# Moving layernorm and merge additions from GpSimd to VectorE, with another order in the third merge

## The chip, the cores and the metric

The kernel runs on one core of a Trainium2 chip. The metric is the device time of one execution in microseconds (us). A core has a matrix engine (TensorE, PE in the profile, with its weight loads as PEld), VectorE (DVE), ScalarE (ACT), GpSimd (POOL) and SyncE (SP), which here only issues transfers. Each engine works through its own queue in order and waits at semaphores for the others. All values are float32. The matrix products use a float32 form that rounds its operands, so the kernel splits each operand into a high and a low part and adds three products (high·high, low·high, high·low).

## The reference

One layer of a recurrent decoder with 512 prompt rows and 32 sample rows, which the kernel treats as 544 columns of one problem. What matters here, with the branches' own recurrences left out:

```
gates  = sigmoid(x @ w_in[gates] + b)                      # 3 branches x 1024
merged = gates[0]*(h_gla @ w_up_gla) + gates[1]*(h_ml @ w_up_ml) + gates[2]*(h_hg @ w_up_hg)
x = LN(2**0.25 * x + merged @ w_out;  ln1)
hid = square(relu(x @ w_ff_up))
x = LN(2**0.25 * x + hid @ w_ff_down; ln2)
LN(x) = (x - mean(x)) * rsqrt(mean((x - mean(x))**2) + 1e-5) * g + b     # over the 1024 channels
```

## The kernel before, in words

Everything is held transposed: channels lie on the 128 partitions, the 544 rows along them. A vector of 1024 channels is thus eight tiles of 128x544 (`KD = 8`), called column tiles below, and a product is computed one output tile at a time: `gemm` (line 160 on) loads the weight tile of 128x1024 by a transfer on SP's queue into `raw` (three buffers), ScalarE copies it to `wh` (line 141), VectorE subtracts to get `wl` (line 142; two buffers each of `wh` and `wl`), and PE runs 8 x 3 x 2 matmuls of 272 columns into one of two PSUM buffers (line 158). So one output tile of a product with 1024 channels is 48 matmuls, one of the third merge (256 channels) is 12, and one of the second feed-forward product (2 x 1024 channels per block) is 96. The `wh` of a product can be written only when the product two before it has stopped reading that buffer.

The inputs of the products are `xh`, `xl` (the layer's input, split), `mh`, `ml` (the merged branches), `x1h`, `x1l` (after the first layernorm) and the tiles `hid*`, `hd*` (the hidden layer). `xh`, `xl`, `x1h` and `x1l` are tiles [128, 8, TX] with TX = 546, so that two extra columns behind the 544 can carry the layernorm's gain and bias through the first feed-forward product; a row of one column tile has 2184 bytes. `mh` and `ml` have rows of 544 values, 2176 bytes.

The order of the instructions is set by a scheduler which simulates the program as it is written and gives some instructions (those under `high_priority`) precedence; each engine then keeps that order.

**Merges** (class `Merge`, lines 840 to 874). For each of eight tiles, `gates` computes a sigmoid gate: product (48 matmuls), bias on VectorE (line 215), three activations on ScalarE (lines 206 to 208). `products` computes the branch's projection; VectorE multiplies it with the gate (line 868) and GpSimd adds it to `merged` (line 872). The first merge writes instead of adding. The third one (line 935 on) computes all eight gates first, then all eight products, and splits each finished tile of `merged` into `mh` (ScalarE) and `ml` (VectorE, line 180), which the output projection reads next.

**Layernorm** (`ln_tile`, line 953). After each tile of the output projection VectorE adds the residual (line 1019 in the first layernorm; 1060 in the second, after the last feed-forward product). The sums over channels run over tiles: `a1` gathers x and `a2` its squares, and a matmul with a constant matrix then sums over the partitions (lines 985 and 992). To keep the numbers small, x is first centred on `cm`. Before the change `cm` is the mean over the first four tiles: GpSimd adds three of them (line 961), VectorE the fourth, a matmul (line 967) takes the mean; only then are the four tiles centred in one go (line 972, VectorE), squared (ScalarE, line 974) and added to `a1` and `a2` on GpSimd (lines 978 and 979). In the first layernorm each centred tile is also written as `x1h` (ScalarE, 1012) and `x1l` (VectorE, 1013) for the feed-forward product. In the second, the last two tiles are handled apart (lines 1063 to 1094) with the columns in two halves: their weights are split beforehand into `lh` and `ll` (line 180), the two tiles are centred before their product is added (line 1075).

**End** (lines 1097 to 1109). For each half of the columns the eight tiles get `ne` added (the negative mean), are multiplied by `rstd`, and get gain and bias. Tuples at the top give some of this to GpSimd (`ADDP`, `MULP`) and VectorE (`AFFD`), the rest to VectorE and ScalarE. Transfers of two tiles each go out on SP's queue. Between the two layernorms, during the first feed-forward product, GpSimd also applies the first layernorm to the residual (lines 1049 and 1050, sixteen additions and multiplications of 128x544).

Of the kernel before, what the change touches and what calls it, by code (L numbers as in the profile page):

```python
# [14 lines left out]
T = 544  # L15
# [4 lines left out]
TX = T + 2  # L20
# [9 lines left out]
ADDP, MULP, AFFD = (5, 6, 7), (7,), (2, 5)  # L30
# [12 lines left out]
def build(tc, I, O):  # L43
    nc = tc.nc
    with ExitStack() as ctx:
# [78 lines left out]
        ones5 = const.tile([128, 128], F32R, name="ones5")  # L124
        nc.gpsimd.memset(ones5.bitcast(F32), 1.0 / 512.0)
# [713 lines left out]
        class Merge:  # L839
# [7 lines left out]
            def gates(self, m0, pl):  # L847
                for m in range(m0, m0 + 4):
# [14 lines left out]
            def products(self, m0):  # L863
                for m in range(m0, m0 + 4):
# [6 lines left out]
                    eng = nc.gpsimd  # L871
                    eng.tensor_tensor(out=merged[:, m, :], in0=merged[:, m, :], in1=g, op=ALU.add)  # L872
# [58 lines left out]
        gb2s, gb2p = pool("gb2", 4)  # L931
# [4 lines left out]
        mr_.gates(0, gbp)  # L936
        mr_.gates(4, gb2p)
        mr_.split()
        mr_.products(0)
        mr_.products(4)  # L940
        gb2s.close()
# [11 lines left out]
        def ln_tile(x, m, sl, last, after):  # L953

            if m == 0:
                return
            if m < 4:
                eng = nc.vector if m == 3 else nc.gpsimd

                to = a1 if m < 3 else ftile("a1r").bitcast(F32R)  # L960
                eng.tensor_tensor(out=to[:, sl], in0=(x[:, 0, sl] if m == 1 else a1[:, sl]), in1=x[:, m, sl], op=ALU.add)  # L961
                if m < 3:
                    return
                for hf in range(2):
                    ps = psr.tile([128, 512], F32, tag="r", name="mu")
                    s = slice(hf * HT, (hf + 1) * HT)
                    nc.tensor.matmul(ps[:, 0:HT], ones5, to[:, s], start=True, stop=True)
                    nc.scalar.activation(out=cm[:, s], in_=ps[:, 0:HT], func=AF.Copy)
                nc.gpsimd.memset(a1, 0.0)
                nc.gpsimd.memset(a2, 0.0)  # L970
            for i in range(0 if m == 3 else m, m + 1):
                nc.vector.tensor_tensor(out=x[:, i, sl], in0=x[:, i, sl], in1=cm[:, sl], op=ALU.subtract)  # L972
                sq = ftile("sq")
                nc.scalar.activation(out=sq[:, sl], in_=x[:, i, sl], func=AF.Square)
                if after:
                    after(i, sl)
                eng = nc.vector if last else nc.gpsimd
                eng.tensor_tensor(out=a1[:, sl], in0=a1[:, sl], in1=x[:, i, sl], op=ALU.add)
                eng.tensor_tensor(out=a2[:, sl], in0=a2[:, sl], in1=sq[:, sl], op=ALU.add)
# [252 lines left out]
```

## Time and profile before

| | us |
|---|---|
| median of 3 runs (lowest, highest) | 968.91 (965.64, 971.26) |
| the profiled execution's own time | 968.76 |
| its span, from the first to the last instruction | 966.9 |
| PE busy | 926.0 (96%) |
| DVE busy | 569.1 (59%) |
| ACT busy | 404.5 (42%) |
| POOL busy | 232.9 (24%) |

The profile counts a matmul as busy from its start to its modelled end, and matmuls overlap: a 272-column matmul is given some 288 ns, but a new one starts about every 125 ns. A stretch in which PE is busy all the time can therefore still differ in how many matmuls it holds, and the useful figure is matmuls per stretch. Time is counted from the first instruction. The third merge's products lie at 472 to 489 us, the output projection and first layernorm at 489 to 549, the feed-forward products at 549 to 955, with the second layernorm from 870 on.

### The profile page before, as it was taken

The page shows a single profiled execution, that of the slowest core. Times are in us where ns is not written, and L with a number is a line of the kernel's source. Part 1 is how long each engine was busy: PE and PEld are TensorE (multiplying, and loading weights), DVE is VectorE, ACT ScalarE, POOL GpSimd, SP SyncE. Part 2 cuts the span into 40 slices and gives each one's busy share as a digit, 9 for nine tenths or more (in the row PEclk, how much of TensorE's full clock was granted, in tenths as well). Part 3 has the DMA queues.
Part 4 walks back from the last instruction along what each step waited for, and adds up shares of the span by engine and source line. Part 5 has one row for each costly group of instructions (what it writes and reads, how often), then busy time and mean ns, then how long its engine had stood idle before and what let it go on. Part 6 is the DMA issues. An engine that isn't in the chain of part 4 may idle for free.

```text
span 966.9 us, 17405 instructions
## 1 busy us (share of the span) xinstructions
PE 926.0 (96%) x7279; PEld 910.7 (94%) x7279; DVE 569.1 (59%) x877; ACT 404.5 (42%) x688; POOL 232.9 (24%) x210
## 2 busy tenths in 40 slices
PE   8999999799999999999989798999999999999795
PEld 7998999799999999999989798999999999999794
DVE  4895467866775676773565855553222455532836
ACT  4386223643555443545523356542111344521414
POOL 0311232643102435120235692000000000001722
PEclk9999999899999999999999899999999999999898
DMA  7321241022132112041144222222222222222202
GB/s 258 118 86 44 84 129 57 16 87 88 60 96 90 49 47 97 25 158 55 33 154 121 79 67 87 88 88 88 87 88 87 88 87 88 88 87 88 85 3 93
DMA packets 37598, 82.73 MB, mean 86 GB/s; under 512 B 12709, under 2 KB 18341, under 8 KB 37521
## 3 DMA queue, kind: packets, MB, share of 16 engines
q1 hardware_dynamic: 25072, 73.28, 23.3%
q10 hardware_dynamic: 12384, 8.33, 3.0%
q8 instruction: 57, 0.93, 0.4%
q14 instruction: 21, 0.16, 0.1%
q0 software_dynamic: 64, 0.02, 0.0%
HBM read 76.51 MB, written 5.09 MB: 84 GB/s over the span
## 4 chain that ended last, share of the span: by engine, by line
PE 86%; DVE 6%; POOL 3%; issue 2%; ACT 1%; DMA 1%; ACTq 0%; DVEq 0%
PE g L158 74%; PE g L83 3%; PE lv L401 2%; POOL merged L1050 2%; POOL merged L1049 1%; DVE wl L142 1%; DVE qe L393 1%; DVE merged L972 1%; PE o L458 1%; DVE x1l L1013 1%; PE oTm L760 1%; PE qkp L673 0%; PE oT L282 0%; DVE ml L180 0%; DMA fw<-in_wfirst 0%
## 5 line engine op out<-in xcount | busy, mean ns | idle before, releaser
L142 DVE TENSOR_TENSOR wl<-raw,wh 128x1024 fp32r<-128x1024 f32 (+2 forms) x139 | 168.4, 1212 | 152.4 <-ACT wh L141 149.6
L141 ACT ACTIVATE wh<-raw 128x1024 fp32r<-128x1024 f32 (+2 forms) x139 | 133.3, 959 | 277.0 <-PE g L158 258.8
L158 PE MATMUL g<-xh,wh 128*128 128x272 f32 x752 | 162.1, 295 | 0.0
L158 PE MATMUL g<-xh,wl 128*128 128x272 f32 x752 | 161.2, 293 | 0.0
L158 PE MATMUL g<-xl,wh 128*128 128x272 f32 x752 | 161.1, 294 | 0.0
L158 PEld LDWEIGHTS g<-xl,wh 128*128 128x128 f32 x752 | 120.8, 191 | 0.9 <-issue 0.5
L158 PEld LDWEIGHTS g<-xh,wh 128*128 128x128 f32 x752 | 121.0, 192 | 0.7 <-issue 0.2
L158 PEld LDWEIGHTS g<-xh,wl 128*128 128x128 f32 x752 | 121.1, 192 | 0.3
L158 PE MATMUL g<-x1h,wh 128*128 128x272 f32 (+1 forms) x512 | 107.1, 290 | 2.9 <-DVE relu L1036 2.9
L158 PE MATMUL g<-x1l,wh 128*128 128x272 f32 (+1 forms) x512 | 106.9, 290 | 0.0
L158 PE MATMUL g<-x1h,wl 128*128 128x272 f32 (+1 forms) x512 | 106.9, 290 | 0.0
L158 PEld LDWEIGHTS g<-x1h,wh 128*128 128x128 f32 x512 | 81.2, 189 | 3.3 <-DVE relu L1036 3.3
L158 PEld LDWEIGHTS g<-x1l,wh 128*128 128x128 f32 x512 | 81.5, 190 | 0.1
L158 PEld LDWEIGHTS g<-x1h,wl 128*128 128x128 f32 x512 | 80.8, 188 | 0.0
L961 POOL TENSOR_TENSOR a<-merged 128x544 f32<-128x544 f32 x2 | 4.8, 2421 | 295.6 <-ACT wh L141 284.3
L158 PE MATMUL g<-hidl,wh 128*128 128x272 f32 x280 | 58.1, 289 | 0.0
L158 PE MATMUL g<-hidh,wh 128*128 128x272 f32 x280 | 57.9, 288 | 0.0
L158 PE MATMUL g<-hidh,wl 128*128 128x272 f32 x280 | 57.8, 288 | 0.0
L1038 ACT ACTIVATE relu<-relu,gw 128x544 f32<-128x544 f32 x32 | 24.0, 750 | 77.2 <-DVE relu L1037 77.2
L872 POOL TENSOR_TENSOR merged<-merged,gb 128x544 f32<-128x544 f32 x16 | 26.8, 1678 | 86.8 <-ACT gb L207 47.8
L215 DVE TENSOR_SCALAR gb<-g,vec 128x544 f32<-128x544 f32 x24 | 18.8, 782 | 45.2 <-PE g L158 45.1
L158 PEld LDWEIGHTS g<-hidl,wh 128*128 128x128 f32 x280 | 44.0, 188 | 0.0
(405 smaller groups left out, 1863.3 us busy)
## 6 DMA issues: line engine op xcount, KB each, us to landing
raw<-in_wff SPq DMA_DIRECT2D x64, 512.0 KB, 3.6
raw<-in_win SPq DMA_DIRECT2D x47, 512.0 KB, 3.2
xr<-in_xT SPq DMA_DIRECT2D x16, 272.0 KB, 3.2
raw<-in_wout SPq DMA_DIRECT2D x8, 512.0 KB, 4.0
out_yT<-merged SPq DMA_DIRECT2D x8, 272.0 KB, 2.4
fw<-in_wfirst ACTq DMA_DIRECT2D x8, 256.0 KB, 5.4
raw<-in_wup_ml SPq DMA_DIRECT2D x8, 192.0 KB, 2.3
raw<-in_wup_gla SPq DMA_DIRECT2D x8, 192.0 KB, 2.4
```

The costliest lines, as they stand in the source:

```text
L83: nc.tensor.matmul(first_ps[i][hf], w[:, i * 128:(i + 1) * 128], a[:, k, hf * HT:(hf + 1) * HT], start=(k == 0 and n == 0), stop=(k == KD ...
L141: nc.scalar.activation(out=h[:, 0:n], in_=raw[:, 0:n], func=AF.Copy)
L142: nc.vector.tensor_tensor(out=l[:, 0:n], in0=raw[:, 0:n], in1=h[:, 0:n].bitcast(F32), op=ALU.subtract)
L158: nc.tensor.matmul(ps[:, hf, 0:w_], w, a(k)[:, hf * HT:hf * HT + w_], start=(k == 0 and s == 0), stop=(k == nk - 1 and s == 2))
L215: nc.vector.tensor_scalar(out, ps, vcol(col), XMIN, ALU.add, ALU.max)
L393: nc.vector.tensor_tensor(out=Q[s, :, p, 0:L // 2].rearrange("p a (n m) -> p a n m", m=m), in0=blk(qv)[s, :, :, m:2 * m], in1=Ev[s, :, :, ...
L401: nc.tensor.matmul(lv[0:R, o:o + 2 * H].rearrange("p (a b) -> p a b", a=2), Kv[:, p, c * R:(c + 1) * R], Q[:, p, :, c * H:(c + 1) * H], st ...
L458: nc.tensor.matmul(o[:, h * dv:(h + 1) * dv], at[:, c * 4 + h, :], vtok[:, cc, h * dv:(h + 1) * dv], start=(h == 0), stop=(cc == 0 and h = ...
L760: nc.tensor.matmul(oT[0:97, h * 32 + 4 * n:h * 32 + 4 * n + 4], Cs[:, n, :], qF[h][:, 4 * n:4 * n + 4], start=False, stop=(h == 3 and n == 7))
L872: eng.tensor_tensor(out=merged[:, m, :], in0=merged[:, m, :], in1=g, op=ALU.add)
L1038: nc.scalar.activation(out=r_, in_=r_, func=AF.Relu, bias=gw[:, 1:2])
L1050: nc.gpsimd.tensor_tensor(out=y, in0=y, in1=rstd, op=ALU.mult)
```

## The change

- Rows: TX goes from 546 to 548, so a row of `xh`, `xl`, `x1h`, `x1l` has 2192 bytes in place of 2184.
- Merges: the addition to `merged` is done by VectorE in place of GpSimd. The third merge computes the gate of tile m+1, then the product of tile m, and so on, in place of eight gates and then eight products. A pool of four more gate buffers goes.
- Layernorms: `cm` is the mean of the first tile alone (ScalarE copies it, a matmul with 1/128 takes the mean). Every tile is centred as soon as it is there. The additions to `a1` and `a2` are done by VectorE; the first tile starts the sums without an addition, so two memsets of GpSimd go.
- End: all additions and multiplications by VectorE, all gains and biases by ScalarE.

```
-TX = T + 2
+TX = T + 4
...
-ADDP, MULP, AFFD = (5, 6, 7), (7,), (2, 5)
+ADDP, MULP, AFFD = (), (), ()
...
-        nc.gpsimd.memset(ones5.bitcast(F32), 1.0 / 512.0)
+        nc.gpsimd.memset(ones7.bitcast(F32), 1.0 / 128.0)
...
-                    eng = nc.gpsimd
-                    eng.tensor_tensor(out=merged[:, m, :], in0=merged[:, m, :], in1=g, op=ALU.add)
+                    nc.vector.tensor_tensor(out=merged[:, m, :], in0=merged[:, m, :], in1=g, op=ALU.add)
...
-        mr_.gates(0, gbp)
-        mr_.gates(4, gb2p)
+        mr_.gates(0, gbp, 1)
         mr_.split()
-        mr_.products(0)
-        mr_.products(4)
-        gb2s.close()
+        for m in range(KD):
+            if m + 1 < KD:
+                mr_.gates(m + 1, gbp, 1)
+            mr_.products(m, 1)
...
-        def ln_tile(x, m, sl, last, after):
+        def ln_tile(x, m, sl, after):

             if m == 0:
-                return
-            if m < 4:
-                eng = nc.vector if m == 3 else nc.gpsimd
-
-                to = a1 if m < 3 else ftile("a1r").bitcast(F32R)
-                eng.tensor_tensor(out=to[:, sl], in0=(x[:, 0, sl] if m == 1 else a1[:, sl]), in1=x[:, m, sl], op=ALU.add)
-                if m < 3:
-                    return
+                xr_ = ftile("a1r").bitcast(F32R)
+                nc.scalar.activation(out=xr_[:, sl], in_=x[:, 0, sl], func=AF.Copy)
                 for hf in range(2):
...
-                    nc.tensor.matmul(ps[:, 0:HT], ones5, to[:, s], start=True, stop=True)
+                    nc.tensor.matmul(ps[:, 0:HT], ones7, xr_[:, s], start=True, stop=True)
                     nc.scalar.activation(out=cm[:, s], in_=ps[:, 0:HT], func=AF.Copy)
-                nc.gpsimd.memset(a1, 0.0)
-                nc.gpsimd.memset(a2, 0.0)
-            for i in range(0 if m == 3 else m, m + 1):
-                nc.vector.tensor_tensor(out=x[:, i, sl], in0=x[:, i, sl], in1=cm[:, sl], op=ALU.subtract)
-                sq = ftile("sq")
-                nc.scalar.activation(out=sq[:, sl], in_=x[:, i, sl], func=AF.Square)
-                if after:
-                    after(i, sl)
-                eng = nc.vector if last else nc.gpsimd
-                eng.tensor_tensor(out=a1[:, sl], in0=a1[:, sl], in1=x[:, i, sl], op=ALU.add)
-                eng.tensor_tensor(out=a2[:, sl], in0=a2[:, sl], in1=sq[:, sl], op=ALU.add)
+            nc.vector.tensor_tensor(out=x[:, m, sl], in0=x[:, m, sl], in1=cm[:, sl], op=ALU.subtract)
+            sq = ftile("sq") if m else a2
+            nc.scalar.activation(out=sq[:, sl], in_=x[:, m, sl], func=AF.Square)
+            if after:
+                after(m, sl)
+            if m:
+                nc.vector.tensor_tensor(out=a1[:, sl], in0=x[:, 0, sl] if m == 1 else a1[:, sl], in1=x[:, m, sl], op=ALU.add)
+                nc.vector.tensor_tensor(out=a2[:, sl], in0=a2[:, sl], in1=sq[:, sl], op=ALU.add)
```

The order of the instructions on VectorE shows what moves. In the third merge (`gb` is the gate tile, `g` the product in PSUM), the end of the products and the start of the output projection stood on VectorE so before, where the additions between multiplication (L868) and split (L180) are GpSimd's and do not appear:

```order
L868 TENSOR_TENSOR gb<-g,gb 128x544
L180 TENSOR_TENSOR ml<-merged,mh 128x544
L142 TENSOR_TENSOR wl<-raw,wh 128x1024
L868 TENSOR_TENSOR gb<-g,gb 128x544
L180 TENSOR_TENSOR ml<-merged,mh 128x544
L142 TENSOR_TENSOR wl<-raw,wh 128x1024
L180 TENSOR_TENSOR ml<-merged,mh 128x544 x2
L1019 SCALAR_TENSOR_TENSOR merged<-xr,g 128x544
```

Now a period of the alternating loop, and its end, stand so (L871 is the addition, L996 the split of the layernorm's gain and bias, L1008 the former L1019):

```order
L215 TENSOR_SCALAR gb<-g,vec 128x544
L142 TENSOR_TENSOR wl<-raw,wh 128x1024
L868 TENSOR_TENSOR gb<-g,gb 128x544
L142 TENSOR_TENSOR wl<-raw,wh 128x256
L871 TENSOR_TENSOR merged<-merged,gb 128x544
L180 TENSOR_TENSOR ml<-merged,mh 128x544
```

```order
L215 TENSOR_SCALAR gb<-g,vec 128x544
L142 TENSOR_TENSOR wl<-raw,wh 128x256
L996 TENSOR_TENSOR x1l<-vec,x1h 128x8 x2
L868 TENSOR_TENSOR gb<-g,gb 128x544
L871 TENSOR_TENSOR merged<-merged,gb 128x544
L142 TENSOR_TENSOR wl<-raw,wh 128x1024 x2
L180 TENSOR_TENSOR ml<-merged,mh 128x544
L868 TENSOR_TENSOR gb<-g,gb 128x544
L871 TENSOR_TENSOR merged<-merged,gb 128x544
L180 TENSOR_TENSOR ml<-merged,mh 128x544
L1008 SCALAR_TENSOR_TENSOR merged<-xr,g 128x544
```

The weights of a gate and of a product now alternate on VectorE, and the addition has its place in the row.

In the first layernorm VectorE's order was, from the moment the mean is there:

```order
L972 TENSOR_TENSOR merged<-merged,cm 128x544 x4
L1019 SCALAR_TENSOR_TENSOR merged<-xr,g 128x544
L142 TENSOR_TENSOR wl<-raw,wh 128x1024
L1013 SCALAR_TENSOR_TENSOR x1l<-merged,vec,x1h 128x544
L972 TENSOR_TENSOR merged<-merged,cm 128x544
L1013 SCALAR_TENSOR_TENSOR x1l<-merged,vec,x1h 128x544 x3
```

Now every tile takes the same six instructions (L1008 residual, L961 centring, weights, L967 and L968 the sums, L1002 the low part):

```order
L1008 SCALAR_TENSOR_TENSOR merged<-xr,g 128x544
L961 TENSOR_TENSOR merged<-merged,cm 128x544
L142 TENSOR_TENSOR wl<-raw,wh 128x1024
L967 TENSOR_TENSOR a_5668<-a_5668,merged 128x544
L968 TENSOR_TENSOR a_5669<-a_5669,sq 128x544
L1002 SCALAR_TENSOR_TENSOR x1l<-merged,vec,x1h 128x544
```

The block of four centrings is gone, and two additions per tile have come from GpSimd.

In the second layernorm VectorE had a block of six centrings, with the weights of the next product behind it:

```order
L1060 TENSOR_TENSOR merged<-merged,g 128x544
L961 TENSOR_TENSOR a1r<-a_5672,merged 128x544
L142 TENSOR_TENSOR wl<-raw,wh 128x1024
L972 TENSOR_TENSOR merged<-merged,cm 128x544 x4
L1075 TENSOR_TENSOR merged<-merged,cm 128x544 x2
L180 TENSOR_TENSOR ll<-raw,lh 128x1024
L142 TENSOR_TENSOR wl<-raw,wh 128x1024
```

Now the centrings begin with the first tile (L1049 is the former L1060, L1064 the former L1075):

```order
L1049 TENSOR_TENSOR merged<-merged,g 128x544
L142 TENSOR_TENSOR wl<-raw,wh 128x1024
L961 TENSOR_TENSOR merged<-merged,cm 128x544
L1064 TENSOR_TENSOR merged<-merged,cm 128x544 x2
L142 TENSOR_TENSOR wl<-raw,wh 128x1024
L1049 TENSOR_TENSOR merged<-merged,g 128x544
L961 TENSOR_TENSOR merged<-merged,cm 128x544
L142 TENSOR_TENSOR wl<-raw,wh 128x1024
L967 TENSOR_TENSOR a_5668<-a_5668,merged 128x544
L968 TENSOR_TENSOR a_5669<-a_5669,sq 128x544
```

Three of the six centrings have moved to the first tile, the others to their own tiles, and the splits of the last weights (`ll`) now stand among the later tiles.

More of the change, by code (lines that the diff above doesn't have):

```diff
@@ L123, in build @@
         nc.gpsimd.memset(epsl, LN_EPS)
-        ones5 = const.tile([128, 128], F32R, name="ones5")
-        nc.gpsimd.memset(ones5.bitcast(F32), 1.0 / 512.0)
+        ones7 = const.tile([128, 128], F32R, name="ones7")
+        nc.gpsimd.memset(ones7.bitcast(F32), 1.0 / 128.0)
         onesn = const.tile([128, 128], F32, name="onesn")
@@ L845, in __init__, with gates @@
                 self.ready = []
-            def gates(self, m0, pl):
-                for m in range(m0, m0 + 4):
+            def gates(self, m0, pl, n=4):
+                for m in range(m0, m0 + n):
                     c = M_G + self.br * KD + m
@@ L861, in split, with products @@
                         split(self.hh[:, k, :], self.hl[:, k, :], self.h[:, k, :])
-            def products(self, m0):
-                for m in range(m0, m0 + 4):
+            def products(self, m0, n=4):
+                for m in range(m0, m0 + n):
                     ps = gemm([(I[self.wup][m], self.nk)], lambda k: self.hh[:, k, :], lambda k: self.hl[:, k, :])
@@ L930, in build @@
         t2s.close()
-        gb2s, gb2p = pool("gb2", 4)
         mps, mp = pool("mp", 1, "right")
@@ L1019, in build @@
             nc.vector.scalar_tensor_tensor(halves(x1[:, m, :]), halves(xr), ALPHA, ps, ALU.mult, ALU.add)
-            ln_tile(x1, m, slice(0, T), m == KD - 1, put_x1)
+            ln_tile(x1, m, slice(0, T), put_x1)
         for hf in range(2):
@@ L1060, in build @@
                     nc.vector.tensor_tensor(out=xm, in0=xm, in1=ps, op=ALU.add)
-                    ln_tile(x1, m, slice(0, T), False, None)
+                    ln_tile(x1, m, slice(0, T), None)
         lh = bigp.tile([128, KD, TX], F32R, tag="big", name="lh").rearrange("p a b -> p (a b)")
```

## Prediction

> **What bounds the kernel now.** I read the page first, then who waited for whom on PE, then the windows of PE by stage, and last the order of time on VectorE and GpSimd at the places found.
>
> ```profile
> span 966.9 us, 17405 instructions
> PE 926.0 (96%) x7279; PEld 910.7 (94%) x7279; DVE 569.1 (59%) x877; ACT 404.5 (42%) x688; POOL 232.9 (24%) x210
> ```
>
> PE is the bound: nothing is won except where PE stands still, where its clock is lowered, or where its matmuls come at a slower pace. The waits of PE (engine, line, releaser: us in all, times, longest):
>
> ```profile
> PE g L158 <- DVE wl L142: 11.0, 5, 5.5
> ...
> PE g L158 <- DVE merged L1019: 3.8, 1, 3.8
> PE g L158 <- DVE relu L1036: 2.9, 2, 1.6
> ```
>
> In the large products PE waits for VectorE, 17.7 us in these eight waits. Where, and what each place costs with the clock, is in the windows (stretch, its length, PE busy, matmuls, granted clock, DMA share, GB/s):
>
> ```profile
> 430.00:472.00 42.00, 42.00 (x333) 1.00 0.15 51
> 497.00:520.00 23.00, 23.00 (x186) 1.00 0.44 128
> 650.00:700.00 50.00, 50.00 (x400) 1.00 0.28 93
> 750.00:850.00 100.00, 100.00 (x789) 1.00 0.27 86
> 472.50:504.50 32.00, 26.84 (x194) 0.95 0.38 117
> 504.50:549.25 44.75, 39.47 (x292) 0.92 0.35 105
> 549.25:591.00 41.75, 38.91 (x298) 1.00 0.21 67
> 870.00:928.00 58.00, 52.48 (x397) 0.94 0.24 74
> 492.40:495.70 3.30, 3.30 (x16) 0.50 0.43 150
> 540.10:546.80 6.70, 5.67 (x25) 0.50 0.35 114
> 912.20:918.90 6.70, 5.91 (x26) 0.50 0.71 224
> ```
>
> An undisturbed stretch (650 to 700) holds 400 matmuls in 50 us, 8.0 per us or 0.125 us each. Measured by that, the third merge with the first two output tiles (472.5 to 504.5) lacks 256 - 194 = 62 matmuls, 7.75 us; the rest of the output projection (504.5 to 549.25) 358 - 292 = 66, 8.25 us; the second layernorm (870 to 928) 464 - 397 = 67, 8.4 us. Together **24.4 us**, the waits and the half-clock stretches behind them, which are the last three rows.
>
> Why VectorE is late there:
>
> ```profile
> 532.71 5.45 DVE L1013 SCALAR_TENSOR_TENSOR x1l<-merged,vec,x1h 128x544 fp32r<-128x544 f32 x3
> 551.84 1.21 DVE L142 TENSOR_TENSOR wl<-raw,wh 128x1024 fp32r<-128x1024 f32 x1
> 552.98 0.71 DVE L978 TENSOR_TENSOR a<-a,merged 128x544 f32<-128x544 f32 x1
> 554.25 0.77 DVE L1013 SCALAR_TENSOR_TENSOR x1l<-merged,vec,x1h 128x544 fp32r<-128x544 f32 x1
> 908.32 2.35 DVE L180 TENSOR_TENSOR ll<-raw,lh 128x1024 fp32r<-128x1024 f32 x1
> 910.59 2.35 DVE L142 TENSOR_TENSOR wl<-raw,wh 128x1024 fp32r<-128x1024 f32 x1
> 538.08 0.71 DVE L1019 SCALAR_TENSOR_TENSOR merged<-xr,g 128x544 f32<-128x544 f32 x1
> 535.77 1.81 POOL L978 TENSOR_TENSOR a<-a,merged 128x544 f32<-128x544 f32 x1
> ```
>
> The same split `x1l` takes 1.82 us while GpSimd adds and 0.77 us when it is idle; `wl` 2.35 and 1.21. Each addition on GpSimd thus delays a VectorE instruction by 1.1 us, more than it would cost on VectorE itself (0.71). Behind the block of four (six) centrings this delays `wl`, and PE stops.
>
> **The change part by part.** The sum goes against the profiled execution's own 968.76 us, of which the span is 966.9; it lies 0.15 under the median.
>
> First layernorm. Per tile VectorE now does residual (0.71, as L1019), centring 0.71, weights 1.21, two sums of 0.71 each and x1l 0.77: 4.8 us, in 48 x 0.125 = 6.0 us of PE. The last of a tile's six ends some 5 us after the tile, before the next one; the weights, third in the row, end about 3 us after it and are wanted after 6. The wait for the mean is 0.5 us of PE work into the third tile plus two ScalarE copies; behind it on VectorE stand the weights of the fifth, wanted 10 us later. At the end `x1l` of tile 8 comes about 5.0 us after it; the feed-forward product reads that tile after seven of eight, 7 x 6 x 0.125 = 5.3 us. This cover is thin (0.3 us), and what it loses PE loses once. Gain **8.25 us**.
>
> Second layernorm. A tile there is 96 matmuls, 12 us; VectorE needs four instructions of 0.71 (residual, centring, two sums), two weights and two `ll` of 1.21, 7.7 us without GpSimd. The two centrings of the last tiles wait for the mean 5 to 6 us into a tile, with weights behind them that are wanted at 12. Gain **8.4 us**.
>
> Third merge. Now every product of 12 matmuls (1.5 us) is followed by a gate whose weights can be converted only from the moment the gate before has been read. How long that takes shows any gate in the trace (first four rows):
>
> ```profile
> 442.00 1.06 ACT L141 ACTIVATE wh<-raw 128x1024 fp32r<-128x1024 f32 x1 [2.90 <-PE g L158]
> 442.06 0.42 PE L158 MATMUL g<-xh,wh 128*128 128x272 f32 x2
> ...
> 442.33 0.78 DVE L215 TENSOR_SCALAR gb<-g,vec 128x544 f32<-128x544 f32 x1 [4.10 <-PE g L158]
> 443.10 1.22 DVE L142 TENSOR_TENSOR wl<-raw,wh 128x1024 fp32r<-128x1024 f32 x1
> ...
> 473.76 0.26 DVE L1007 TENSOR_TENSOR x1l<-vec,x1h 128x8 fp32r<-128x8 f32 x2
> 476.37 0.43 DVE L142 TENSOR_TENSOR wl<-raw,wh 128x256 fp32r<-128x256 f32 x1
> 478.53 1.56 DVE L142 TENSOR_TENSOR wl<-raw,wh 128x256 fp32r<-128x256 f32 x1
> ```
>
> The gate before ended at 442.06, `wl` at 444.32, 2.26 us later. Today a gate of 6 us covers that; then only 1.5 us of product and four matmuls that need `wh` alone, 2.0 us. So PE stands 0.3 us at each of the six product-to-gate changes, 1.8 us. At the end, the output projection's first `wl` stands behind the bias (0.78), a small `wl` (0.43), two tiny ones (0.26), L868 and the new L871 (0.71 each, like L978) from 0.27 us after the last gate: 3.15, plus 1.22 gives 4.4, wanted at 3.0 + 0.5. That is 0.9 us more. So 2.7 of the 7.75 us stay lost; gain **5.05 us**, between 0 (each stall 1.3 us, if ScalarE's sigmoids come first) and 7.75. `ml` of the last tile is then done about 9 us after the last gate and wanted near 11.
>
> The additions of the second merge, eight times 0.71 us, go onto VectorE amid the last recurrence. GpSimd's held it up as much: of the last two rows the second, 1.1 us longer, ran beside an addition. I put this at 0, with 0.5 either way.
>
> Row length. Gates over `xh` come at 333 in 42 us, 0.1261 each; products over rows of 2176 bytes at 0.1250 (650 to 700) or 0.1237 (497 to 520). The 2256 gate-type matmuls could gain 1.1 ns each, 2.5 us. The 1536 over `x1h` come at 0.1267; half of them are two columns wider, 0.5 ns on the mean, so 1.2 ns each, 1.9 us. Between 0 and 4.4 us; four of the eight tiles start at a multiple of 16 bytes already with 2184, and all eight with 2192, so I take half, **2.2 us**.
> The Trainium skill ("SBUF — State Buffer", section "SBUF: two separate sides") gives SBUF lines of 16 bytes and a price for each new line. By an estimate from that page a half of 1088 bytes touches 69 lines in place of 68 when it starts 8 bytes off, 1.5%, 1.8 ns on half of 3792 matmuls, 3.5 us in place of 2.2; no run here shows it yet.
>
> End.
>
> ```profile
> 955.59 4.02 DVE L1099 TENSOR_TENSOR merged<-merged,ne 128x272 f32<-128x272 f32 x5
> 959.53 2.54 DVE L1103 TENSOR_TENSOR merged<-merged,rstd 128x272 f32<-128x272 f32 x7
> ...
> 960.00 3.14 ACT L1107 ACTIVATE merged<-merged,vec 128x272 f32<-128x272 f32 x6 [3.31 <-DVE merged L1103]
> ```
>
> Five additions took 4.0 us beside GpSimd; alone they go at the multiplications' 0.35 us, eight in 2.9. So ScalarE starts 1.0 us earlier but has eight instead of six steps of 0.5: it ends at 963.0 in place of 963.1. **0.1 us**.
>
> The feed-forward start keeps GpSimd's sixteen instructions; of its 41.75 us (549 to 591) about 3 stay lost, the two waits for L1036.
>
> Sum: 8.25 + 8.4 + 5.05 + 2.2 + 0.1 = 24.0. 968.76 - 24.0 = 944.8, and 945 against the median.
>
> **The rivals.**
> *The third merge gives nothing back.* ScalarE's queue holds sigmoids and `mh` ahead of the next `wh`, and six stalls of 0.3 become 1.0 or more. For it: any lateness of `wh` passes to `wl` in full. Against it: in the gate quoted ScalarE had idled 2.90 us before its `wh`, and `mh` adds 0.7. The time is 945 + 5 = **950**. If the stalls also lower the clock, the price is up to 1.7 us each time: the first half-clock row (16 matmuls in 3.3 us, half the pace) follows on waits of which the longest is the one in brackets:
>
> ```profile
> 491.37 0.52 PE L158 MATMUL g<-mh,wl 128*128 128x272 f32 x2 [2.08 <-DVE wl L142]
> ```
>
> The Trainium skill ("TensorE: Matmul & The Clock Gate", section "Why this matters for your kernels") lets the clock fall only after idle gaps over about 3 us; by it such stalls never would, while our rows show it after waits of 2.1 us at most, 5.2 us idle in the 32 us from 472.5 on. I give the clock's part 3 in 100.
>
> *Rows pay in full and the merge runs without a stall*: 4.4 and 7.75 in place of 2.2 and 5.05, **940**. Against it: a `wl` that would have to be 0.3 us faster than in any gate.
>
> *Slower: VectorE is slow for another reason than GpSimd*, for instance the traffic of transfers (105 to 224 GB/s there), and the moved additions cost 1.82 us each. Then a tile of the first layernorm needs 0.71 + 2.35 + 4 x 1.82 = 10.3 us against 6.0, 30 us lost over seven tiles in place of 8.25: with the other two places unchanged and the rows' gain, about 968.8 + 22 - 2 = **988**. It decides from (6.0 - 0.71 - 1.21)/4 = 1.02 us per addition on. Against it: at 553 us the same addition took 0.71 us, in the same code.
>
> *The change does not free VectorE in the second layernorm*, because the six `wl` and `ll` crowd into the last two tiles: half of 8.4 stays, **949**. Against it: 24 us for 4 `ll`, 4 `wl` and some eight short ones, 15 us.
>
> **How the numbers follow.** Forecast 0.72 (own range 941 to 949), merge gives nothing 0.12, full rows 0.07, second layernorm crowded 0.06, slower 0.03. The range of 80%, 938.5 to 951, takes in the unknown costs and the 6 us between the shown runs. No more than half a per cent, about what a measurement of this kernel can tell from no change, would need 19 us of 24 to be missing: 0.02; slower 0.03; faster 0.95.
>
> **What would show it.** In the profile after: PE's waits for `wl` of 1 us and more are gone at the merge, the output projection and the second layernorm, six of 0.2 to 0.4 us at the gates come in; no half-clock stretch after 400 us but the last; x1l and the sums at 0.7 to 0.8 us; 333 gate matmuls in about 41.7 us; the two waits for L1036's successor unchanged. The forecast is wrong if the additions on VectorE take over 1 us, or if the windows of the three places still lack over 25 matmuls each.

## The result: 942.1 us in place of 967.3, and where the time went

The changed kernel takes 942.12 us (median of 4 runs, 940.62 to 943.7); the kernel before, run beside it, 967.27. The ratio is 0.9735, with a 95% interval of 0.9697 to 0.9773: faster, by 25 us. The prediction was 945.0, range 938.5 to 951.

### The profile after

The page and the waits of PE in the changed kernel (engine, line, releaser: us in all, times, longest), to be held against the lines of before in the prediction:

```profile
span 940.1 us, 17333 instructions
PE 915.7 (97%) x7279; PEld 900.0 (96%) x7279; DVE 556.2 (59%) x917; ACT 406.9 (43%) x694; POOL 141.7 (15%) x152
```
```profile
PE g L158 <- DVE relu L1025: 3.1, 2, 1.6
PE g L158 <- DVE wl L142: 1.8, 8, 0.7
```

PE's waits for `wl` have gone from 11.0 us to 1.8, none longer than 0.7; the waits for L1019 and L868 are gone; that for the first feed-forward product is as it was. VectorE has 40 instructions more and is busy 13 us less.

The windows of PE at the same places (stretch, its length, PE busy, matmuls, granted clock, DMA share, GB/s): third merge, rest of the output projection, start of the feed-forward products, second layernorm.

```profile
441.00:485.00 44.00, 42.62 (x329) 1.00 0.26 87
495.00:540.00 45.00, 45.00 (x359) 1.00 0.45 132
545.00:585.00 40.00, 36.85 (x291) 1.00 0.25 79
855.00:910.00 55.00, 55.00 (x440) 1.00 0.25 77
```

At 8 matmuls per us the first lacks 23, 2.9 us; the second 1; the third 29, 3.6 us; the fourth none. The clock is 1.00 in all four, where it had been 0.92 to 0.95 at the merge and the layernorms.

Since both programs run the same 7279 matmuls, the start of the n-th matmul in the one trace can be taken from that in the other. The difference, in us, grows like this:

| matmul | place | before | after | ahead by |
|---|---|---|---|---|
| 3400 | last recurrence | 434.57 | 431.60 | 2.97 |
| 4000 | merge and first output tiles done | 518.23 | 510.50 | 7.73 |
| 4100 | output projection | 530.81 | 523.06 | 7.75 |
| 4200 | first layernorm over | 551.71 | 535.62 | 16.09 |
| 5000 | first feed-forward product over | 657.58 | 640.87 | 16.71 |
| 5700 | before its second block | 745.47 | 728.77 | 16.70 |
| 6500 | after its second block | 847.17 | 829.53 | 17.64 |
| 6900 | before the second layernorm | 897.40 | 879.77 | 17.63 |
| 7100 | after it | 930.93 | 904.88 | 26.05 |
| 7200 | last sums | 944.17 | 918.12 | 26.05 |
| | end of the span | 966.86 | 940.09 | 26.77 |

So the first layernorm gave 8.3 us, the second 8.4, the merge 4.8 with the faster rows in it. The rest, 5.2 us, came in small steps wherever `xh` or `x1h` is read, and at the end. Of single runs the first 100 us differ by up to 4 us from one to the next (at matmul 800 the runs below stand between 3.2 us behind and 0.7 ahead of the profiled execution of before, whatever their edit). So steps in this table count for the places behind matmul 3200.

### The profile page after: what moved, and what is told of

It reads as the page before. It is cut to its first block, busy times and chain, and to the rows that moved or that the text cites. A ratio compares the mean times of both kernels' runs of the same rounds, so it can differ in the third digit from the quotient of the medians.

```text
span 940.1 us, 17333 instructions
## 1 busy us (share of the span) xinstructions
PE 915.7 (97%) x7279; PEld 900.0 (96%) x7279; DVE 556.2 (59%) x917; ACT 406.9 (43%) x694; POOL 141.7 (15%) x152
## 3 DMA queue, kind: packets, MB, share of 16 engines
q10 hardware_dynamic: 12384, 8.33, 3.0%
## 4 chain that ended last, share of the span: by engine, by line
PE 85%; DVE 5%; POOL 4%; ACT 3%; issue 1%; DMA 1%; POOLq 0%; ACTq 0%; DVEq 0%
PE g L158 73%; PE lv L401 3%; PE g L83 2%; DVE wl L142 2%; POOL merged L1039 1%; POOL merged L1038 1%; ACT wh L141 1%; DVE qe L393 1%; PE o L458 1%; POOL cvo L583 1%; PE oTm L760 1%; PE qkp L673 0%; PE oT L282 0%; DMA fw<-in_wfirst 0%; PE sp L689 0%
## 5 line engine op out<-in xcount | busy, mean ns | idle before, releaser
L142 DVE TENSOR_TENSOR wl<-raw,wh 128x1024 fp32r<-128x1024 f32 (+2 forms) x139 | 158.3, 1140 | 142.8 <-ACT wh L141 140.4
L1027 ACT ACTIVATE relu<-relu,gw 128x544 f32<-128x544 f32 x32 | 24.0, 750 | 77.2 <-DVE relu L1026 77.2
L158 PEld LDWEIGHTS g<-hidh,wl 128*128 128x128 f32 x280 | 43.9, 188 | 0.0
L158 PEld LDWEIGHTS g<-hidh,wh 128*128 128x128 f32 x280 | 43.8, 188 | 0.0
```

The source lines that it names most:

```text
L142: nc.vector.tensor_tensor(out=l[:, 0:n], in0=raw[:, 0:n], in1=h[:, 0:n].bitcast(F32), op=ALU.subtract)
L158: nc.tensor.matmul(ps[:, hf, 0:w_], w, a(k)[:, hf * HT:hf * HT + w_], start=(k == 0 and s == 0), stop=(k == nk - 1 and s == 2))
L1027: nc.scalar.activation(out=r_, in_=r_, func=AF.Relu, bias=gw[:, 1:2])
```

## The experiments

The theory on record: GpSimd's additions hold up VectorE's instructions, behind a block of centrings this makes the weights late, and PE stands. The rivals: the block does it alone; contention does it alone; the gain comes from other edits (rows, order of the merge).

### Rows alone, and a row length that is wrong in another way

```
 # kernel before
-TX = T + 2
+TX = T + 4
```

> The kernel before with nothing changed but the row length of xh, xl, x1h and x1l (2192 bytes in place of 2184). The two traces show the products over xh and x1h 1.25 ns per matmul faster after the change. Theory: the row length alone does that; 3792 matmuls x 1.25 ns = 4.7 us, so 964.1 us against the profiled 968.76, and the windows of PE over a gate stretch hold 8.0 matmuls per us in place of 7.93; the waits for wl stay as before (11 us in 5). Rival (the half taken in the prediction): 2.2 us, 966.6. Rival 2: the pace comes from something else in the change (less traffic on the other engines), and the matmuls stay at 0.1261 and 0.1267 us: 968.8.

Measured: 961.6 us against 967.16, ratio 0.9948 (0.993 to 0.9965), a gain of 3.4 to 6.8 us. PE's waits for `wl` stay (10.7 us). Not all that its profiled execution gains is pace: between matmuls 3800 and 4000, which read none of the longer rows, it gains 1.5 us, because the half-clock stretch after 492.40 in the kernel before is missing, although PE has waited there just as long (2.10 us in place of 2.08):

```profile
487.66 0.52 PE L158 MATMUL g<-mh,wl 128*128 128x272 f32 x2 [2.10 <-DVE wl L142]
488.80:492.10 3.30, 3.30 (x29) 1.00 0.42 142
```

Another 1.1 us comes in the second layernorm, where the wait for `wl` is as long as before and the half-clock stretch starts 3.4 us ahead of its end in place of 0.9.

```
 # changed kernel
-TX = T + 4
+TX = T + 6
```

> The changed kernel with rows of 2200 bytes in place of 2192 (TX = T + 6). 2200 is longer still, but as 2184 it is a multiple of 8 and not of 16, so that every second column tile starts 8 bytes off a multiple of 16. Theory (the start of the rows decides): the products over xh and x1h go back to 0.1261 and 0.1267 us per matmul, 4.7 us: 946.8 us. Rival (any length but 2184 is good, or the pace came from another edit): 942.1, 0.125 and 0.1257 us per matmul.

Measured: 944.13 us (943.79 to 945.39), 2.0 us over the changed kernel, where the theory had 4.7; ratio to before 0.9754 (0.9726 to 0.9782). The windows of PE in the second block of the first feed-forward product, in this order: before (2184 bytes), the kernel before with 2192, and the changed kernel with 2200; and in front of the second of them the gate stretch that had held 333 matmuls.

```profile
760.00:835.00 75.00, 75.00 (x592) 1.00 0.27 85
```
```profile
427.00:469.00 42.00, 42.00 (x337) 1.00 0.16 51
752.00:827.00 75.00, 75.00 (x598) 1.00 0.30 91
```
```profile
747.00:822.00 75.00, 75.00 (x593) 1.00 0.28 85
```

2192 bytes hold 598 matmuls in 75 us, with none of the other edits; 2184 and 2200 hold 592 and 593. Counted over the same 600 matmuls (numbers 5800 to 6400) the stretch takes 76.34 us before and 75.57 after, 1.3 ns each; over all undisturbed output tiles it is 1.25 ns with 2184 and 1.0 ns with 2200. So the pace comes from the row length, and from its place to 16 bytes, not from being longer. 1.25 ns on 3792 matmuls is 4.7 us, where the prediction took 2.2; 1.0 ns would be 3.8, of which the times with 2200 bytes show 2.0, and the early stages, in which single runs differ by up to 4 us, can hide the rest. The Trainium skill ("SBUF — State Buffer", "Specifications (TRN2)") charges each crossing to a new line of 16 bytes; the estimate made from it in the prediction, 3.5 us, lies nearer to it than the half; the trace agrees in sign, and the size is larger.

### The layernorms: block or contention

Three kernels, each the kernel before with one part of the layernorm's change.

```
 # layernorms of the change alone: first-tile mean, every tile centred at once, sums on VectorE
-            if m < 4:
...
-            for i in range(0 if m == 3 else m, m + 1):
-                nc.vector.tensor_tensor(out=x[:, i, sl], in0=x[:, i, sl], in1=cm[:, sl], op=ALU.subtract)
...
+            nc.vector.tensor_tensor(out=x[:, m, sl], in0=x[:, m, sl], in1=cm[:, sl], op=ALU.subtract)
...
+                nc.vector.tensor_tensor(out=a1[:, sl], in0=x[:, 0, sl] if m == 1 else a1[:, sl], in1=x[:, m, sl], op=ALU.add)
+                nc.vector.tensor_tensor(out=a2[:, sl], in0=a2[:, sl], in1=sq[:, sl], op=ALU.add)
```

> The kernel before with the layernorms of the change alone (centring on the first tile's mean, every tile centred at once, the sums on VectorE). Theory: all that the two layernorms gave in the whole change comes from here, 8.3 us in the first and 8.4 in the second, 16.7 together: 952.1 us, ratio 0.983, and the big waits for wl at 493 us stay while those at 530 and 905 us go. Rival: part of it needs the other edits (the merge leaves its stall and the half clock behind it as a burden on the first layernorm), then under 12 us: above 956.

Measured: 950.18 us, ratio 0.9842 (0.9814 to 0.9869). By the count of matmuls the first layernorm gives 8.33 us and the second 8.42, as in the whole change.

```
 # the same, with the sums back on GpSimd
+                eng = nc.vector if last else nc.gpsimd
-                nc.vector.tensor_tensor(out=a1...
-                nc.vector.tensor_tensor(out=a2...
+                eng.tensor_tensor(out=a1...
+                eng.tensor_tensor(out=a2...
```

> As the run with the layernorms alone, but the sums a1 and a2 stay on GpSimd (the last tile of the first layernorm on VectorE, as before). It parts the two edits: no block of centrings, but GpSimd still adds beside VectorE. Theory of the prediction, contention by itself sets it: x1l and wl stay at 1.8 and 2.3 us beside the additions, and most of the 16.7 us stays lost: at least 962. Rival, the block sets it: a tile then holds 0.71 + 0.71 + 1.21 + 0.77 + 2 x 1.1 us of delay = 5.6 us of VectorE in 6.0 of PE, with nothing queued in front of the weights, so the stalls go although the instructions stay slow: 952 to 955.

Measured: 952.28 us, ratio 0.9856 (0.9835 to 0.9877). The first layernorm gives 8.33 us, the second 8.42: the same to 0.01. Yet VectorE is still held up. One tile's row there, in order of time on VectorE (start, duration), and GpSimd beside it:

```profile
525.49 0.72 DVE L1011 SCALAR_TENSOR_TENSOR merged<-xr,g 128x544 f32<-128x544 f32 x1 [1.61 <-PE g L158]
526.24 0.72 DVE L963 TENSOR_TENSOR merged<-merged,cm 128x544 f32<-128x544 f32 x1
526.89 1.22 DVE L142 TENSOR_TENSOR wl<-raw,wh 128x1024 fp32r<-128x1024 f32 x1
528.39 1.52 DVE L1005 SCALAR_TENSOR_TENSOR x1l<-merged,vec,x1h 128x544 fp32r<-128x544 f32 x1 [0.29 <-ACT x1h L1004]
531.51 0.72 DVE L1011 SCALAR_TENSOR_TENSOR merged<-xr,g 128x544 f32<-128x544 f32 x1 [1.60 <-PE g L158]
```
```profile
527.11 2.22 POOL L970 TENSOR_TENSOR a<-a,merged 128x544 f32<-128x544 f32 x1 [2.01 <-DVE merged L963]
529.29 1.84 POOL L971 TENSOR_TENSOR a<-a,sq 128x544 f32<-128x544 f32 x1
```

`x1l` takes 1.52 us in place of 0.77, but the row ends with 1.6 us of idle time before the next tile, and `wl` is in front of the delay. So contention is there and costs nothing.

```
 # kernel before, block kept, all of the layernorm's additions on VectorE
-                eng = nc.vector if m == 3 else nc.gpsimd
+                eng = nc.vector
...
-                eng = nc.vector if last else nc.gpsimd
+                eng = nc.vector
```

> The kernel before with its mean over four tiles and its block of centrings, but all additions of the layernorm (those for the mean, and those to a1 and a2) on VectorE. Theory of the prediction, contention sets it: x1l 0.77 and wl 1.21 us throughout and most of the 16.7 us comes back: 952 to 957. Rival, the block sets it: behind the mean VectorE has 0.71 + 4 x 0.71 + 8 x 0.71 + 4 x 0.77 + 1.21 us = 13.5 us of work in a tile of 6.0, more than with GpSimd, so PE still stands behind the block: 962 to 970. If both runs come out at 952 to 957, either edit is enough alone and the loss needs both.

Measured: 954.44 us, ratio 0.9873 (0.9858 to 0.9889). The two layernorms again give 8.33 and 8.44 us, with the block in place. But the start of the feed-forward product loses 4.6 us of it:

```profile
494.00:539.00 45.00, 45.00 (x360) 1.00 0.42 124
539.00:575.00 36.00, 33.10 (x234) 0.91 0.22 69
555.20:562.00 6.80, 5.86 (x26) 0.50 0.51 154
```
```profile
556.14 0.82 PE L158 MATMUL g<-x1h,wh 128*128 128x272 f32 x2 [2.90 <-DVE relu L1036]
```

The additions queue up behind the block until the last tile, so the sums over channels come 11.2 us after the start of that product (6.2 in the changed kernel). Its first tiles need them before they can leave PSUM, so PE waits 2.9 us, and 6.8 us at half the clock come with it.

What follows: in the kernel before, VectorE is late with the weights only because the block and the contention come together; either edit takes that away. With the block alone 4.6 of the 16.8 us are lost again at the start of the feed-forward product; with GpSimd's additions alone nothing is. The change does both. But contention by itself costs nothing only while a tile's row still fits, as the next run shows.

```
 # changed kernel, and on GpSimd, for each centred tile, two additions that nothing reads
+            nc.gpsimd.tensor_tensor(out=ne[:, sl], in0=cm[:, sl], in1=x[:, m, sl], op=ALU.add)
+            nc.gpsimd.tensor_tensor(out=rstd[:, sl], in0=cm[:, sl], in1=sq[:, sl], op=ALU.add)
```

> The changed kernel, with two more additions per centred tile on GpSimd in both layernorms, into tiles that are overwritten later (work that nothing needs). It sets the suspected contention beside the full row of VectorE instructions: per tile 4.8 us alone, and 2 x 1.1 us of delay. Theory (contention and the amount of work decide together, and what counts is whether a tile's row fits into its product): 7.0 us in the first layernorm against 6.0 of PE, so VectorE falls behind by 1 us per tile and PE loses 3 to 7 us there, x1l and the sums at 1.8 us again; in the second, 7.7 + 2.2 = 9.9 us fit into 12 and nothing is lost: 945 to 949 us. Rival (GpSimd's additions only harm behind a block): 942.1.

Measured: 948.27 us (947.96 to 951.28), ratio to before 0.981 (0.977 to 0.9851), 6 us over the changed kernel (7 by the two ratios). The first layernorm and the start of the feed-forward product lose 7.8 us by the count of matmuls, the second layernorm none:

```profile
512.00:546.00 34.00, 29.90 (x228) 1.00 0.35 103
870.00:915.00 45.00, 45.00 (x360) 1.00 0.27 83
```

One tile's row on VectorE there, up to the centring of the next, and GpSimd beside it:

```profile
523.25 0.72 DVE L961 TENSOR_TENSOR merged<-merged,cm 128x544 f32<-128x544 f32 x1
523.89 1.22 DVE L142 TENSOR_TENSOR wl<-raw,wh 128x1024 fp32r<-128x1024 f32 x1
525.02 1.89 DVE L969 TENSOR_TENSOR a<-a,merged 128x544 f32<-128x544 f32 x1
526.84 1.88 DVE L970 TENSOR_TENSOR a<-a,sq 128x544 f32<-128x544 f32 x1
528.64 0.78 DVE L1004 SCALAR_TENSOR_TENSOR x1l<-merged,vec,x1h 128x544 fp32r<-128x544 f32 x1
529.34 0.71 DVE L1010 SCALAR_TENSOR_TENSOR merged<-xr,g 128x544 f32<-128x544 f32 x1
530.08 0.73 DVE L961 TENSOR_TENSOR merged<-merged,cm 128x544 f32<-128x544 f32 x1
```
```profile
524.11 2.21 POOL L966 TENSOR_TENSOR ne<-cm,merged 128x544 f32<-128x544 f32 x1 [2.82 <-DVE merged L961]
526.30 1.84 POOL L967 TENSOR_TENSOR rstd<-cm,sq 128x544 f32<-128x544 f32 x1
```

A period is 530.08 - 523.25 = 6.83 us, where the sum had said 7.0; PE's tile would need 6.0. VectorE has no gap, and PE waits 0.5 us or more in each tile (1.06, 0.55, 0.53 and 0.51), then 1.4 us each for `x1h` and for the sums at the end. The delay falls on the two sums; `x1l`, for which 1.8 us had been expected, keeps its 0.78. This is the rule in its plainest form: the row of one tile, with the delays in it, fits into the tile's product or it does not.

### The third merge: order or engine

```
 # kernel before, order only (additions stay on GpSimd)
-            def gates(self, m0, pl):
+            def gates(self, m0, pl, n=4):
...
-        gb2s, gb2p = pool("gb2", 4)
...
-        mr_.gates(0, gbp)
-        mr_.gates(4, gb2p)
+        mr_.gates(0, gbp, 1)
         mr_.split()
-        mr_.products(0)
-        mr_.products(4)
-        gb2s.close()
+        for m in range(KD):
+            if m + 1 < KD:
+                mr_.gates(m + 1, gbp, 1)
+            mr_.products(m, 1)
```

> The kernel before with the alternating third merge alone (gate of tile m+1, then product of tile m); the additions stay on GpSimd. In the two traces the third merge and the start of the output projection gave 4.8 us, of which six stalls of 0.3 us at the gates are the price. Theory: the order gives it, since in a period of 8 us VectorE holds some 4.6 us and one delay of 1.1 does not matter: 964.0 us, with six waits of 0.1 to 0.4 us for wl at the gates and no half-clock stretch at 490 us. Rival: GpSimd's addition delays bias or wl at each gate by 1.1 us, then six stalls of 1.4: 969 or more.

Measured: 963.61 us against 968.18, ratio 0.9945 (0.9926 to 0.9964). The merge is 3.9 us shorter by the count of matmuls, with six stalls of 0.31 us at the gates, one wait of 1.43 at the output projection and no half clock; 0.2 of it is lost in the first layernorm.

```
 # kernel before, engine only (old order)
-                    eng = nc.gpsimd
+                    eng = nc.vector
```

> The kernel before with the additions of the second and third merge on VectorE and the old order (eight gates, then eight products). In a product of 1.5 us VectorE has then the multiplication 0.71, the weights 0.43, the addition 0.71 and the split 0.72: 2.6 us, 1.1 more than PE, 8.6 us late over eight products. Theory (the order decides): no gain, 968 to 972, and PE still waits over 3 us for wl at the start of the output projection. Rival (GpSimd's contention decides): the waits there go and 4 to 7 us come back, 962 to 965.

Measured: 963.23 us, ratio 0.9941 (0.9916 to 0.9966); the merge is 4.6 us shorter, and the first layernorm 0.7. Of both merge runs' gain some 1.5 us is the half-clock stretch in the profiled execution of before, which is missing in the run with the rows alone too, where the waits are unchanged; the rest comes from the waits. The theory named first there fell, the rival holds. The last products on VectorE, and the stretch that answers 472.5 to 504.5 of before:

```profile
481.37 0.72 DVE L180 TENSOR_TENSOR ml<-merged,mh 128x544 fp32r<-128x544 f32 x1
482.01 0.73 DVE L872 TENSOR_TENSOR merged<-merged,gb 128x544 f32<-128x544 f32 x1
482.64 0.72 DVE L868 TENSOR_TENSOR gb<-g,gb 128x544 f32<-128x544 f32 x1
483.28 1.22 DVE L142 TENSOR_TENSOR wl<-raw,wh 128x1024 fp32r<-128x1024 f32 x1
```
```profile
468.50:500.50 32.00, 29.71 (x230) 1.00 0.45 133
```

230 matmuls in place of 194 and no half clock. VectorE does run late (2.6 us of work in a product of 1.5), but some of the additions and low parts are put off until after the products, and the two things on which PE waits, the multiplication that frees PSUM and the weights, come between them at 0.7 and 0.4 us. PE still waits twice for a multiplication (0.51 and 1.23 us, the second for the one at 482.64). With GpSimd the same small weights had taken 1.56 us.

So here too each edit alone gives most of what both give. In the changed kernel the alternation gives nothing beyond the engine; it adds the stalls that the prediction counted. One of them, in order of time:

```profile
442.69 0.41 PE L158 MATMUL g<-xl,wh 128*128 128x272 f32 x2
443.27 0.52 PE L158 MATMUL g<-xh,wl 128*128 128x272 f32 x2 [0.16 <-DVE wl L142]
```

From start to start 0.58 us in place of 0.25, 0.33 lost, the same at 435.31, 451.23, 459.19, 467.15 and 475.11: six in all.

### The two waits left, and a faster kernel

```
 # changed kernel, first block (blk == 0), after each of its sixteen tiles m
-                if blk == 0 and 2 <= m < 2 + KD:
-                    y = x1[:, m - 2, :]
-                    nc.gpsimd.tensor_tensor(out=y, in0=y, in1=ne, op=ALU.add)
-                    nc.gpsimd.tensor_tensor(out=y, in0=y, in1=rstd, op=ALU.mult)
-                    nc.scalar.activation(out=y, in_=y, func=AF.Identity, ...)
+                if blk == 0:
+                    y = x1[:, m // 2, :]
+                    one = fp.tile([128, 1], F32, tag="one", name="one", bufs=3)
+                    nc.gpsimd.tensor_scalar(one, gw[:, 0:1], 0.0, 1.0, ALU.mult, ALU.add)
+                    nc.vector.scalar_tensor_tensor(y, y, one, ne if m % 2 == 0 else rstd, ALU.mult, ALU.add if m % 2 == 0 else ALU.mult)
+                    if m % 2:
+                        nc.scalar.activation(out=y, in_=y, func=AF.Identity, ...)
```

> The changed kernel, with the first layernorm's residual (sixteen additions and multiplications on GpSimd at the start of the first feed-forward product) given to VectorE, one per output tile over sixteen tiles; a tiny GpSimd instruction of one column makes each wait for its tile. Theory: PE's two waits for L1025 there (start to start 1.85 and 1.87 us in place of 0.25) come from ScalarE's queue, which stands at L1040 for GpSimd's slow additions with the next weights behind it; without them PE gains 3.2 us: 938.9 us. VectorE then has 1.22 + 0.77 + 3 x 0.72 = 4.2 of 6.1 us per tile. Rival: the waits belong to the layernorm's end (the tiles that wait for ne and rstd) and stay: 942.1, or more if the sixteen instructions delay the weights.

Measured: 938.9 us (937.76 to 941.01), ratio to before 0.97 (0.967 to 0.973). The waits are gone, and the count of matmuls gives 3.7 us at this place. In the changed kernel the chain had been (ScalarE, VectorE, PE, in order of time):

```profile
562.57 0.84 ACT L1040 ACTIVATE merged<-merged,vec 128x544 f32<-128x544 f32 x1 [0.96 <-POOL merged L1039]
563.32 0.73 ACT L1027 ACTIVATE relu<-relu,gw 128x544 f32<-128x544 f32 x1
563.96 1.04 ACT L141 ACTIVATE wh<-raw 128x1024 fp32r<-128x1024 f32 x1
565.03 1.22 DVE L142 TENSOR_TENSOR wl<-raw,wh 128x1024 fp32r<-128x1024 f32 x1 [3.72 <-ACT wh L141]
566.18 0.77 DVE L1025 SCALAR_TENSOR_TENSOR relu<-ne,gw,g 128x544 f32<-128x544 f32 x1
567.01 0.52 PE L158 MATMUL g<-x1h,wh 128*128 128x272 f32 x2 [1.56 <-DVE relu L1025]
```

ScalarE stands at L1040 for GpSimd, behind it L1027 and the weights, behind those `wl` and L1025, which frees the PSUM buffer. With the work spread the same stretch holds 319 matmuls in place of 291:

```profile
545.00:585.00 40.00, 40.00 (x319) 1.00 0.30 93
```

The last three kernels have this edit and vary the merge and the rows.

```
 # old order of the merge, additions on VectorE
+        gb2s, gb2p = pool("gb2", 4)
...
-        mr_.gates(0, gbp, 1)
+        mr_.gates(0, gbp)
+        mr_.gates(4, gb2p)
...
+        mr_.products(0)
+        mr_.products(4)
+        gb2s.close()
```

> The changed kernel with the spread residual (938.9 us) and the third merge put back into its old order (eight gates, then eight products), the additions staying on VectorE. By the two merge runs either edit alone gives about the whole gain of the place: 3.7 us for the order alone, 5.3 for VectorE's additions in the old order, 4.8 for both in the changed kernel. Theory (the alternation is not needed once the additions are on VectorE, and costs its six stalls): 0.5 us faster than with it, 938.4. Rival (the gain of that run was of another origin, and eight products crowd VectorE by 8.6 us): 942 or more.

Measured: 937.7 us (936.1 to 939.76), ratio 0.9695 (0.9655 to 0.9735). By the count of matmuls the place is 0.2 us shorter than with the alternation: no difference that the times can tell, and not the 4 us of the rival.

```
 # pairs: two gates, then the two products before
-        mr_.gates(0, gbp, 1)
+        mr_.gates(0, gbp, 2)
         mr_.split()
...
+        for m in range(0, KD, 2):
+            if m + 2 < KD:
+                mr_.gates(m + 2, gbp, 2)
+            mr_.products(m, 2)
```

> The changed kernel with the spread residual (938.9 us) and the third merge in pairs: two gates, then the two products before. Three of the six stalls of 0.33 us at the change from product to gate go, 1.0 us; at the end four products follow each other, with 4 x 2.6 us of VectorE in 6.0 us of PE, which can hold up the output projection by up to 1.5 us more. Theory: 937.9 to 938.9, with three stalls of 0.33 us left. Rival (the stall comes at every change of tile): six stalls stay.

Measured: 937.09 us (936.06 to 938.22), ratio 0.9688 (0.965 to 0.9726), the lowest median of all, though the runs beside it overlap with it. By the count of matmuls the place is 0.5 us shorter. The stalls are not those of the theory: PE's waits for `wl` fall from seven to four, but only two changes from product to gate are left, and each loses 0.87 us in place of 0.33. Against the changed kernel's 940.62 to 943.7 its runs do not overlap; most of that is the spread residual.

```
 # pairs, and
-TX = T + 4
+TX = T + 16
```

> As the run with pairs, with rows of 2240 bytes (a multiple of 64) in place of 2192 (of 16). In the changed kernel the products over x1h take 752 to 755 ns for six matmuls on most tiles, but 762 on two; over mh, with rows of 2176 bytes (also a multiple of 64), 752 to 755 on all. Theory 1 (multiples of 16 are enough): no change, 0.1257 us per matmul over x1h. Theory 2 (more alignment gives more): the two tiles come down by 8 ns per six, 0.3 ns per matmul on 3792 matmuls, 1 us.

Measured: 937.19 us (937.1 to 937.69), ratio 0.969 (0.9646 to 0.9734), the same. 75 us of the first feed-forward product hold 598 matmuls as with 2192. The tiles differ among themselves in another way (six matmuls over `x1h` take 741 to 767 ns, with 2192 751 to 763), and the mean comes down by 0.1 ns per matmul over `x1h` and 0.2 over `xh`, some 0.6 us in all, which the times cannot tell. A multiple of 16 gives all but that.

## Why the prediction was right, and where it was not

The sum had 24.0 us; the profiled executions differ by 968.76 - 942.1 = 26.7.

| step | forecast | measured |
|---|---|---|
| first layernorm | 8.25 | 8.34 |
| second layernorm | 8.4 | 8.42 |
| third merge | 5.05 | 4.8, of which some 0.5 from rows (counted there) |
| rows | 2.2 | 4.7 |
| end | 0.1 | 0.7 |
| rest | 0 | 0.2 |

**Layernorms.** Right in place and size. The groups of VectorE in the first one show the durations forecast, 0.7 to 0.8:

```profile
L1002 DVE SCALAR_TENSOR_TENSOR x1l<-merged,vec,x1h 128x544 fp32r<-128x544 f32 x8 | 6.2, 780 | 0.0
L968 DVE TENSOR_TENSOR a<-a,sq 128x544 f32<-128x544 f32 x7 | 5.0, 719 | 0.0
L967 DVE TENSOR_TENSOR a<-a,merged 128x544 f32<-128x544 f32 x6 | 4.3, 718 | 0.0
```

They do so beside transfers of 132 GB/s, more than before, which ends the rival of slow additions by traffic. The thin cover of 0.3 us for `x1l` held: no wait stands there. Of the cause the prediction was too narrow in one point: it counted 1.1 us for each addition of GpSimd as if it had to be paid, and the run with the sums on GpSimd paid 0.75 us for two and lost nothing of PE's time.

**Merge.** Six stalls of 0.3 us and 0.9 at the output projection were forecast; six of 0.33 and one of 0.87 show. Luck has a part in the size: the 7.75 us from which the prediction started hold 1.5 us of a half-clock stretch, which is missing in the run with the rows alone, with the same waits. Against such an execution the merge would give some 3.3 us. That the changed order was needed for the gain was taken for granted, and the run with the engine alone shows it was not. The rival that the merge gives nothing back, and that its stalls lower the clock, did not come.

**Rows.** The step that failed: "so I take half". The window prices were already means over all eight tiles, so four tiles at a multiple of 16 bytes are no ground for halving them. Those four are not free either: with 2184 bytes six matmuls over `x1h` take 762 ns on average on the even tiles, which are aligned, and 764 on the odd; with 2192, 757 and 754. Why the aligned tiles lose 5 ns stays open. The full price read from the windows, 4.4, was the better value, 4.7 came.

**End.** ScalarE's last step was forecast as 963.0 in place of 963.1, and against the last sums it is 0.1 us earlier than before; what was left out are the transfers behind it. Before and after, SP's last four (start of the first, time over which they are issued):

```profile
961.14 2.43 SPq L1109 DMA_DIRECT2D out_yT<-merged  x4
```
```profile
933.97 3.40 SPq L1098 DMA_DIRECT2D out_yT<-merged  x4
932.83 4.14 ACT L1096 ACTIVATE merged<-merged,vec 128x272 f32<-128x272 f32 x8 [2.18 <-DVE merged L1092]
```

They are issued over 3.4 us in place of 2.4 and start earlier against the end: from ScalarE's end to the end of the span it is 940.09 - 936.97 = 3.1 us, before 966.86 - 963.14 = 3.7. That the last transfer then finds an emptier queue is a reading that was not tested. That the edit of the end gives the 0.7 us is shown by the other runs: from matmul 7200 to the end of the span, the kernels with rows, layernorms or merge alone stay within 0.04 us of before, and all those that hold the whole change are 0.7 shorter.

**The feed-forward start** kept its two waits, 3.1 us, as forecast, and the run with the spread residual shows their cause.

## What to carry to other kernels

When an engine beside the bound is late, add up its row of instructions over one period of the bound's work, with the delays as the trace shows them, and compare with the period: in the first layernorm 5 of 6 us cost nothing and 6.8 of 6 cost every period. Work that nothing waits for yet can be put off, as at the end of the third merge, and does not count. Two edits that each take away a necessary condition do not add, so run each alone before keeping both. A row length that is off a multiple of 16 bytes is cheap to look for: count matmuls per stretch where PE never waits.

## What the runs showed of the hardware that was not expected

VectorE and GpSimd do not share, they take turns by whole instructions. In the run with needless additions (rows above) GpSimd's first ends at 524.11 + 2.21 = 526.32, and VectorE's L969, started at 525.02, ends at 526.91, 0.59 later; GpSimd's next ends at 528.14, L970 at 528.72, 0.58 later. `wl` began before GpSimd's and kept its 1.22 us; there GpSimd's took 2.21, where one of this shape takes 1.37 with VectorE idle (changed kernel, 562.49 us). The Trainium skill ("SBUF — State Buffer", "Who interferes with whom") calls it an exclusive lock, and the trace agrees. It also names two inputs in SBUF as the condition for VectorE, and that shows too: with GpSimd at work throughout, L1025, which reads `g` from PSUM, takes 0.77 us, and the next instruction but one, L1026 with both operands in SBUF, 1.87 (changed kernel, GpSimd and VectorE in order of time):

```profile
542.53 14.04 POOL L1038 TENSOR_TENSOR merged<-merged,ne 128x544 f32<-128x544 f32 x8 [148.85 <-ACT ne L985]
550.34 0.77 DVE L1025 SCALAR_TENSOR_TENSOR relu<-ne,gw,g 128x544 f32<-128x544 f32 x1
551.03 1.19 DVE L180 TENSOR_TENSOR hdw<-relu,hdh 128x544 fp32r<-128x544 f32 x1
552.15 1.87 DVE L1026 TENSOR_TENSOR relu<-relu,rstd 128x544 f32<-128x544 f32 x1
```

And the clock: the length of a single wait does not decide. Waits of 1.56 and 1.58 us left it at 1.00 (the stretch 545 to 585 after), one of 2.08 was followed by 3.4 us at half, and with one of 2.90 came 6.8 us. But in the run with the rows alone a wait of 2.10 at the same place left it at 1.00, and in the changed kernel one of 1.31 at 334 us came with 6.8 us at half. What else decides is not shown here; gains of 1 to 2 us read from a single trace can be its doing.
